# One-hot terms made on Pool, row pairs and more whole-block loads in a softmax-minus-one-hot kernel

## The chip, the cores and the metric

One core of a Trainium2 chip runs the whole program. The metric is device time in microseconds (us), the median of several executions of one compiled kernel; lower is better. The engines named here are VectorE (DVE), ScalarE (ACT), GpSimd (Pool), SyncE (SP, which only issues loads here) and the sixteen DMA engines that move data between HBM, where the inputs and outputs lie, and SBUF, the core's own memory of 128 partitions. PSUM is a second, smaller memory of the core. TensorE does two tiny transposes and plays no part. A "row" below is a tile row: 128 partitions of 8192 fp32 values, 4.19 MB. There are 64 of them, in 32 blocks of two.

## The reference

```python
logits: (8, 1024, 8192) float32;  labels: (8, 1024) int
logits_max = np.max(logits, axis=-1, keepdims=True)
exp_logits = np.exp(logits - logits_max)
softmax = exp_logits / np.sum(exp_logits, axis=-1, keepdims=True)
one_hot[batch_idx, seq_idx, labels] = 1.0
return (softmax - one_hot).astype(np.float32)
```

The kernel reads 268.5 MB and writes 268.4 MB. Both are needed by any kernel that goes over the data once.

## The kernel before

Three slots of SBUF hold one block each. SP issues loads and ACT issues stores; a load waits until the stores of the block that had its slot are done. Per row, DVE takes the maximum, ACT the exponential with its sum, DVE the reciprocal, ACT scales the whole row, and DVE subtracts "column number equals label", reading the column numbers from PSUM. The letter string says which blocks come as two one-row loads (r) and which as one whole load (w).

```python
G = 2
SLOTS = 3
LOADS = "rrrrrwwwwwwwwwwwwwwwwwwwwwrrrrrr"
# ... (set-up cut)
for t in range(T):
    x = row(t)
    label = lab[:, t % G, t // G : t // G + 1]
    w = run(nc.scalar, [w_max], act, "activation",
            out=x, in_=x, func=Act.Exp, bias=m[:, t : t + 1], scale=1.0, accum_out=s[:, t : t + 1])
    w_sum = run(nc.vector, [w], dve, "reciprocal", out=r[:, t : t + 1], in_=s[:, t : t + 1])
    if t + 1 < T:
        if (t + 1) % G == 0:
            load((t + 1) // G)
        w_max = row_max(t + 1)              # DVE: the next row's maximum
    if t > 0:
        store(t - 1)
    n = 1 if t + 1 < T else 2               # the last row in two halves
    # ... (cols: n equal slices of the row)
    scaled = [run(nc.scalar, [w_sum], act, "activation",
                  out=x[:, c], in_=x[:, c], func=Act.Copy, bias=0.0, scale=r[:, t : t + 1]) for c in cols]
    for c, w in zip(cols, scaled):
        w = run(nc.vector, [w], dve, "scalar_tensor_tensor",
                out=x[:, c], in0=iota[:, c], scalar=label, in1=x[:, c],   # iota lies in PSUM
                op0=Alu.is_equal, op1=Alu.subtract, reverse1=True)
    finished.append(w)
```

## Time and profile before

| | before |
|---|---|
| time, median of the first 3 runs (lowest to highest) | 1248.09 us (1247.36 to 1248.12) |
| span of the profiled execution | 1245.6 us |
| bytes moved, mean rate | 536.98 MB, 431 GB/s |
| busy: DVE, ACT, Pool | 1115.9, 919.0, 7.4 us |

The lines behind this table are in the prediction below. One part of the page is kept for a comparison later: the DMA issues, with the median time from issue to landing at the end of each line.

```profile
out_dram<-X ACTq DMA_DIRECT2D x64, 4096.0 KB, 30.9
X<-in_logits_dram SPq DMA_DIRECT2D x22, 4096.0 KB, 27.5
X<-in_logits_dram SPq DMA_DIRECT2D x21, 33.2
```

A store of one row needs 9.7 us of the sixteen engines at 434 GB/s, yet it lands after 30.9. The rest is queueing: this is what a transfer-bound kernel looks like from the side of one transfer.

### The profile page before, as it was taken

How to read it: one execution, taken by the hardware profiler on the slowest of the kernel's cores; microseconds unless marked ns; L12 is line 12 of the kernel's file. 1: busy time of each engine (PE TensorE's matmuls, PEld its weight loads, DVE VectorE, ACT ScalarE, POOL GpSimd, SP SyncE). 2: the span in 40 equal slices, each digit the busy share in tenths (PEclk: the TensorE clock that was granted, in tenths of full speed). 3: DMA queues.
4: the chain of work that ended last, by engine and by line, in shares of the span. 5: the costliest groups of instructions: out<-in, count | busy, mean ns of one | idle time of the engine just before them, and what ended most of it. 6: DMA issues, size and time to landing. Idle time of an engine off the chain costs nothing.

```text
span 1245.6 us, 592 instructions
## 1 busy us (share of the span) xinstructions
PE 0.4 (0%) x2; PEld 0.3 (0%) x2; DVE 1115.9 (90%) x196; ACT 919.0 (74%) x194; POOL 7.4 (1%) x7
## 2 busy tenths in 40 slices
PE   0000000000000000000000000000000000000000
PEld 0000000000000000000000000000000000000000
DVE  4999997888988889888898888988889999999893
ACT  3888886678767787767867678777777788887772
POOL 2000000000000000000000000000000000000000
DMA  9999999999999999999999999999999999999998
GB/s 398 427 428 432 437 436 441 436 431 425 426 438 448 432 416 440 431 436 438 426 446 437 418 434 432 435 437 442 425 427 438 430 429 437 435 431 431 436 434 388
DMA packets 15460, 536.98 MB, mean 431 GB/s; under 512 B 1728, under 2 KB 1728, under 8 KB 1760
## 3 DMA queue, kind: packets, MB, share of 16 engines
q1 hardware_dynamic: 6240, 268.50, 50.0%
q10 hardware_dynamic: 9216, 268.44, 49.9%
q14 instruction: 4, 0.03, 0.0%
HBM read 268.50 MB, written 268.44 MB: 431 GB/s over the span
## 4 chain that ended last, share of the span: by engine, by line
DMA 60%; DVE 37%; ACT 1%; DVEq 0%; issue 0%; ACTq 0%; SPq 0%
DMA X<-in_logits_dram 32%; DMA out_dram<-X 28%; DVE m L68 19%; DVE X L68 18%; ACT X L68 1%; DVEq L56 0%; DVE r L68 0%; ACTq L68 0%; SPq L223 0%; SPq L56 0%
## 5 line engine op out<-in xcount | busy, mean ns | idle before, releaser
L68 DVE TENSOR_REDUCE m<-X 128x1 f32<-128x8192 f32 x64 | 555.2, 8674 | 108.5 <-DMA X<-in_logits_dram 108.5
L68 ACT ACTIVATE X<-X,m 128x8192 f32<-128x8192 f32 x64 | 455.8, 7122 | 190.2 <-DVE m L68 190.2
L68 DVE SCALAR_TENSOR_TENSOR X<-iota,lab,X 128x8192 f32<-128x8192 int16 (+1 forms) x65 | 559.6, 8611 | 4.1 <-ACT X L68 4.1
L68 ACT ACTIVATE X<-X,r 128x8192 f32<-128x8192 f32 (+1 forms) x65 | 456.0, 7016 | 115.4 <-DVE r L68 115.4
L68 ACT ACTIVATION_READ_ACCUMULATOR X<-X,m 128x1 f32 x64 | 12.0, 187 | 0.0
L68 DVE RECIPROCAL r<-s 128x1 f32<-128x1 f32 x64 | 9.8, 153 | 1.7 <-ACT X L68 1.7
L68 POOL IOTA X<- 128x8192 int16 x1 | 6.9, 6943 | 0.0
L68 DVE TENSOR_SCALAR iota<-X 128x4096 int32<-128x4096 int32 x1 | 4.4, 4428 | 0.1
L68 ACT ACT_TABLE_LOAD x1 | 1.3, 1283 | 0.9 <-SPq L56 0.9
L68 DVE COPY lab<-iota 128x64 f32<-128x64 f32 x1 | 0.2, 225 | 0.5 <-PE iota L68 0.5
L68 PE MATMUL iota<-ident,lab_f 32*128 32x32 f32 x2 | 0.4, 299 | 22.4 <-DVE lab_f L68 22.4
L68 DVE CAST lab_f<-lab_raw 32x256 f32<-32x256 int32 x1 | 0.4, 363 | 0.0
L68 PEld LDWEIGHTS iota<-ident,lab_f 32*128 32x128 f32 x2 | 0.3, 193 | 22.4 <-DVE lab_f L68 22.4
L68 POOL TENSOR_SCALAR_AFFINE_SELECT ident<-ident 32x32 f32<-32x32 f32 x1 | 0.2, 203 | 0.1
L68 POOL MEMSET ident<- 32x32 f32 x1 | 0.1, 115 | 0.5 <-SPq L56 0.5
L212 POOL MEMSET const-bfloat16-1.0<- 128x1 bf16 x1 | 0.1, 106 | 0.0
L212 POOL MEMSET const-uint8-127<- 128x1 uint8 x1 | 0.1, 106 | 0.0
L212 POOL MEMSET const-float32-0.0<- 128x1 f32 x1 | 0.1, 103 | 0.2 <-issue 0.2
L212 POOL MEMSET const-float32-1.0<- 128x1 f32 x1 | 0.1, 103 | 0.0
## 6 DMA issues: line engine op xcount, KB each, us to landing
out_dram<-X ACTq DMA_DIRECT2D x64, 4096.0 KB, 30.9
X<-in_logits_dram SPq DMA_DIRECT2D x22, 4096.0 KB, 27.5
X<-in_logits_dram SPq DMA_DIRECT2D x21, 33.2
lab_raw<-in_labels_dram SPq DMA_DIRECT2D x1, 64.0 KB, 12.3
```

Of the source, the lines that this page charges most:

```text
L68: instruction = getattr(engine, method)(**operands)
L212: nc = _bacc.Bacc("TRN2", target_bir_lowering=False, num_devices=1)
```

## The change

Its intent is to take work from ACT and to shorten a row's way from load to store. Pool makes, ahead of time, the one-hot terms (0 or 1, one byte) of 6144 of the 8192 columns. One DVE pass then scales these columns and subtracts the terms at once, so ACT scales only the other 2048 columns, which DVE finishes as before. Rows are handled in pairs, both maxima first. More blocks are loaded whole, labels load on ACT's queue, and the set-up tiles borrow space of the third slot.

```diff
+HOT = 6144
+CHUNK = 1024
-LOADS = "rrrrrwwwwwwwwwwwwwwwwwwwwwrrrrrr"
+LOADS = "rrwwwwwwwwwwwwwwwwwwwwwwwwwwwrrr"
+    chunk_iota = const.tile([P, CHUNK], i16)
+    hot = const.tile([P, 2, HOT], mybir.dt.uint8)
 ... (set-up cut)
+        def row_hot(t):
+            for k in range(0, HOT, CHUNK):
+                first = [w_chunk, w_turned] if t == 0 else [w_used[t - 2]] if t > 1 else []
+                w = run(nc.gpsimd, first if k == 0 else [], pool, "tensor_scalar",
+                    out=hot[:, t % 2, k : k + CHUNK], in0=chunk_iota[:],
+                    scalar1=float(k), scalar2=label(t), op0=Alu.add, op1=Alu.is_equal)
+            w_hot[t] = w
 ...
+        def row_finish(t, w_exp):
+            w_sum = run(nc.vector, [w_exp], dve, "reciprocal", ...)
+            w_rest = run(nc.scalar, [w_sum], act, "activation",
+                out=x[:, rest], in_=x[:, rest], func=Act.Copy, bias=0.0, scale=r[:, t : t + 1])
+            w_used[t] = run(nc.vector, [w_hot[t], w_sum], dve, "scalar_tensor_tensor",
+                out=x[:, hot_cols], in0=x[:, hot_cols], scalar=r[:, t : t + 1], in1=hot[:, t % 2, :],
+                op0=Alu.mult, op1=Alu.subtract)
+            finished[t] = run(nc.vector, [w_rest], dve, "scalar_tensor_tensor",
+                out=x[:, rest], in0=iota[:], scalar=label(t), in1=x[:, rest],
+                op0=Alu.is_equal, op1=Alu.subtract, reverse1=True)
 ...
+        for b in range(B):
+            load(b)
+            row_hot(b * G)
+            row_hot(b * G + 1)
+            t = b * G
+            row_max(t)
+            row_max(t + 1)
+            if t > 0:
+                store(t - 1)
+            w = row_exp(t)
+            row_finish(t, w)
+            w = row_exp(t + 1)
+            store(t)
+            row_finish(t + 1, w)
```

More of the change, by code (lines that the diff above doesn't have):

```diff
@@ L10 @@
 SLOTS = 3
-LOADS = "rrrrrwwwwwwwwwwwwwwwwwwwwwrrrrrr"
-STORES = "rrrrrrrrrrrrrrrrrrrrrrrrrrrrrrrr"
+HOT = 6144
+CHUNK = 1024
+LOADS = "rrwwwwwwwwwwwwwwwwwwwwwwwwwwwrrr"
 @with_exitstack
@@ L36 @@
     B = T // G
+    REST = V - HOT
     lab_bp = labels.rearrange("a b -> (a b)").rearrange("(b q) -> b q", q=G * P)
@@ L45 @@
     X = const.tile([P, SLOTS, G, V], fp32)
-    lab_raw = const.tile([B, G * P], labels.dtype)
-    lab_f = const.tile([B, G, P], fp32)
-    ident = const.tile([B, B], fp32)
     lab = const.tile([P, G, B], fp32)
     m, s, r = (const.tile([P, T], fp32, name=n) for n in ("m", "s", "r"))
-    iota = psum.tile([P, V], i16)
+    chunk_iota = const.tile([P, CHUNK], i16)
+    hot = const.tile([P, 2, HOT], mybir.dt.uint8)
+    iota = psum.tile([P, REST], i16)
     lab_ps = iota[:].bitcast(fp32)[:, :T].rearrange("p (j b) -> p j b", j=G)
-    with tc.tile_critical():
+    early = X[:, SLOTS - 1, 0, :]
+    lab_raw = early.bitcast(labels.dtype)[:B, : G * P]
+    at = G * P * mybir.dt.size(labels.dtype) // 4
+    lab_f = early[:B, at : at + G * P].rearrange("b (p j) -> b j p", j=G)
+    ident = early[:B, at + G * P : at + G * P + B]
+    made = X[:, SLOTS - 1, G - 1, :].bitcast(i16)[:, :REST]
+    with tc.tile_critical(no_gpsimd_drain=True):
         sem = tc.alloc_semaphore
-        got = [[sem(f"got{i}{q}") for q in range(2)] for i in range(SLOTS)]
-        put = [[sem(f"put{i}{q}") for q in range(2)] for i in range(SLOTS)]
+        got = [[sem(f"got{i}{j}") for j in range(G)] for i in range(SLOTS)]
+        put = [[sem(f"put{i}{j}") for j in range(G)] for i in range(SLOTS)]
         lab_got, dve, act, pe, pool = (sem(n) for n in ("lab_got", "dve", "act", "pe", "pool"))
@@ L74, in run @@
             return counter, count[counter.name]
-        every, rows = slice(0, P), slice(0, G)
-        PIECES = {
-            "r": [(every, slice(j, j + 1)) for j in range(G)],
-            "h": [(slice(i, P, 2), rows) for i in range(2)],
-            "w": [(every, rows)],
-        }
-        def meets(a, b):
-            sets = [[set(range(*d.indices(n))) for d, n in zip(p, (P, G))] for p in (a, b)]
-            return all(x & y for x, y in zip(*sets))
-        loaded, stored, finished = {}, {}, []
@@ L91 @@
-        last_made = []
-        def load(b, behind_first=lambda: None):
-            loaded[b] = []
-            before = stored.get(b - SLOTS, last_made if b == SLOTS - 1 else [])
-            for q, piece in enumerate(PIECES[LOADS[b]]):
-                ps, js = piece
-                free = [w for other, w in before if meets(piece, other)]
-                w = run(
-                    nc.sync, free, got[b % SLOTS][q], "dma_start",
-                    out=X[ps, b % SLOTS, js, :], in_=x_b[b, ps, js, :],
-                )
-                loaded[b].append((piece, w))
-                if q == 0:
-                    behind_first()
@@ L107, in store @@
-        def store(t):
-            b, j = divmod(t, G)
-            stored.setdefault(b, [])
-            for q, piece in enumerate(PIECES[STORES[b]]):
-                ps, js = piece
-                if js.stop != j + 1:
-                    continue
-                w = run(
-                    nc.scalar, [finished[t]], put[b % SLOTS][q], "dma_start",
-                    out=o_b[b, ps, js, :], in_=X[ps, b % SLOTS, js, :],
-                )
-                stored[b].append((piece, w))
-        def row(t):
-            return X[:, t // G % SLOTS, t % G, :]
@@ L124, in row_max @@
-        def row_max(t):
-            b, j = divmod(t, G)
-            arrived = [w for piece, w in loaded[b] if meets(piece, (every, slice(j, j + 1)))]
-            return run(
-                nc.vector, arrived, dve, "tensor_reduce",
-                out=m[:, t : t + 1], in_=row(t), axis=mybir.AxisListType.X, op=Alu.max, negate=True,
-            )
-        w_raw = []
-        load(0, lambda: w_raw.append(run(nc.sync, [], lab_got, "dma_start", out=lab_raw[:], in_=lab_bp)))
-        w_max = row_max(0)
@@ L136 @@
-        w = run(nc.gpsimd, [], pool, "memset", ap=ident[:], constant=0.0)
+        w_raw = run(nc.scalar, [], lab_got, "dma_start", out=lab_raw, in_=lab_bp)
+        w = run(nc.gpsimd, [], pool, "memset", ap=ident, constant=0.0)
         w_ident = run(
             nc.gpsimd, [w], pool, "affine_select",
-            out=ident[:], in_=ident[:], compare_op=Alu.not_equal, fill=1.0,
+            out=ident, in_=ident, compare_op=Alu.not_equal, fill=1.0,
             base=0, pattern=[[-1, B]], channel_multiplier=1,
@@ L141 @@
         )
-        made = X[:, SLOTS - 1, G - 1, :].bitcast(i16)[:, :V]
         w_made = run(
-            nc.gpsimd, [], pool, "iota", out=made, pattern=[[1, V]], base=0, channel_multiplier=0
+            nc.gpsimd, [], pool, "iota",
+            out=made, pattern=[[1, REST]], base=HOT, channel_multiplier=0,
+        )
+        w_chunk = run(
+            nc.gpsimd, [], pool, "iota",
+            out=chunk_iota[:], pattern=[[1, CHUNK]], base=0, channel_multiplier=0,
         )
         step = mybir.dt.size(labels.dtype) // 4
-        lab32 = lab_raw[:].bitcast(i32).rearrange("b (p j s) -> b j p s", j=G, s=step)
@@ L149 @@
-        w_lab = run(nc.vector, w_raw, dve, "tensor_copy", out=lab_f[:], in_=lab32[:, :, :, 0])
+        lab32 = lab_raw.bitcast(i32).rearrange("b (p j s) -> b j p s", j=G, s=step)
+        w_lab = run(nc.vector, [w_raw], dve, "tensor_copy", out=lab_f, in_=lab32[:, :, :, 0])
         for j in range(G):
@@ L152 @@
                 nc.tensor, [w_ident, w_lab], pe, "transpose",
-                out=lab_ps[:, j, :], in_=lab_f[:, j, :], identity=ident[:],
+                out=lab_ps[:, j, :], in_=lab_f[:, j, :], identity=ident,
             )
@@ L159, with load @@
         )
-        last_made.append(((every, slice(G - 1, G)), w_iota))
-        for t in range(T):
+        loaded, stored, finished = {}, {}, {}
+        def load(b):
+            i = b % SLOTS
+            parts = [slice(0, G)] if LOADS[b] == "w" else [slice(j, j + 1) for j in range(G)]
+            for q, js in enumerate(parts):
+                rows = [b * G + j for j in range(*js.indices(G))]
+                free = [stored[t - SLOTS * G] for t in rows] if b >= SLOTS else []
+                free += [w_iota] if b == SLOTS - 1 else []
+                w = run(
+                    nc.sync, free, got[i][q], "dma_start", out=X[:, i, js, :], in_=x_b[b, :, js, :]
+                )
+                loaded.update((t, w) for t in rows)
@@ new lines, in store, with row, label @@
+        def store(t):
+            b, j = divmod(t, G)
+            i = b % SLOTS
+            stored[t] = run(
+                nc.scalar, [finished[t]], put[i][j], "dma_start", out=o_b[b, :, j, :], in_=X[:, i, j, :]
+            )
+        def row(t):
+            return X[:, t // G % SLOTS, t % G, :]
+        def label(t):
+            return lab[:, t % G, t // G : t // G + 1]
+        w_max, w_sum, w_hot, w_used = {}, {}, {}, {}
+        def row_hot(t):
+            for k in range(0, HOT, CHUNK):
+                first = [w_chunk, w_turned] if t == 0 else [w_used[t - 2]] if t > 1 else []
+                w = run(
+                    nc.gpsimd, first if k == 0 else [], pool, "tensor_scalar",
+                    out=hot[:, t % 2, k : k + CHUNK], in0=chunk_iota[:],
+                    scalar1=float(k), scalar2=label(t), op0=Alu.add, op1=Alu.is_equal,
+                )
+            w_hot[t] = w
@@ L164, with row_max, row_exp @@
+        def row_max(t):
+            w_max[t] = run(
+                nc.vector, [loaded[t]], dve, "tensor_reduce",
+                out=m[:, t : t + 1], in_=row(t), axis=mybir.AxisListType.X, op=Alu.max, negate=True,
+            )
+        def row_exp(t):
             x = row(t)
-            label = lab[:, t % G, t // G : t // G + 1]
-            w = run(
-                nc.scalar, [w_max], act, "activation",
+            return run(
+                nc.scalar, [w_max[t]], act, "activation",
@@ L168 @@
                 out=x, in_=x, func=Act.Exp, bias=m[:, t : t + 1], scale=1.0, accum_out=s[:, t : t + 1],
             )
-            w_sum = run(nc.vector, [w], dve, "reciprocal", out=r[:, t : t + 1], in_=s[:, t : t + 1])
-            if t + 1 < T:
-                if (t + 1) % G == 0:
-                    load((t + 1) // G)
-                w_max = row_max(t + 1)
+        def row_finish(t, w_exp):
+            x = row(t)
+            hot_cols, rest = slice(0, HOT), slice(HOT, V)
+            w_sum = run(nc.vector, [w_exp], dve, "reciprocal", out=r[:, t : t + 1], in_=s[:, t : t + 1])
+            w_rest = run(
+                nc.scalar, [w_sum], act, "activation",
+                out=x[:, rest], in_=x[:, rest], func=Act.Copy, bias=0.0, scale=r[:, t : t + 1],
+            )
+            w_used[t] = run(
+                nc.vector, [w_hot[t], w_sum], dve, "scalar_tensor_tensor",
+                out=x[:, hot_cols], in0=x[:, hot_cols], scalar=r[:, t : t + 1], in1=hot[:, t % 2, :],
+                op0=Alu.mult, op1=Alu.subtract,
+            )
+            finished[t] = run(
+                nc.vector, [w_rest], dve, "scalar_tensor_tensor",
+                out=x[:, rest], in0=iota[:], scalar=label(t), in1=x[:, rest],
+                op0=Alu.is_equal, op1=Alu.subtract, reverse1=True,
+            )
@@ L175 @@
+        for b in range(B):
[5 more added lines that the diff above has]
+            row_max(t + 1)
             if t > 0:
                 store(t - 1)
-            n = 1 if t + 1 < T else 2
-            cols = [slice(i * V // n, (i + 1) * V // n) for i in range(n)]
-            scaled = [
-                run(
-                    nc.scalar, [w_sum], act, "activation",
-                    out=x[:, c], in_=x[:, c], func=Act.Copy, bias=0.0, scale=r[:, t : t + 1],
-                )
-                for c in cols
-            ]
@@ L187 @@
-            for c, w in zip(cols, scaled):
-                w = run(
-                    nc.vector, [w], dve, "scalar_tensor_tensor",
-                    out=x[:, c], in0=iota[:, c], scalar=label, in1=x[:, c],
-                    op0=Alu.is_equal, op1=Alu.subtract, reverse1=True,
-                )
-            finished.append(w)
+            w = row_exp(t)
[3 more added lines that the diff above has]
+            row_finish(t + 1, w)
         store(T - 1)
-        for b in range(B - SLOTS, B):
-            for _, w in stored[b]:
-                nc.scalar.wait_ge(*w)
+        for t in range(T - SLOTS * G, T):
+            nc.sync.wait_ge(*stored[t])
```

## The prediction

> **What bounds the kernel now.** I read, in this order: the page's busy shares, its 40 slices, the two DMA queues, the chain that ended last, the groups by line, the waits of the queue that issues the loads, and the windows of the two ends. The busy shares mislead, because VectorE (DVE) leads them with 90%:
>
> ```profile
> PE 0.4 (0%) x2; PEld 0.3 (0%) x2; DVE 1115.9 (90%) x196; ACT 919.0 (74%) x194; POOL 7.4 (1%) x7
> DMA  9999999999999999999999999999999999999998
> DMA packets 15460, 536.98 MB, mean 431 GB/s; under 512 B 1728, under 2 KB 1728, under 8 KB 1760
> q1 hardware_dynamic: 6240, 268.50, 50.0%
> q10 hardware_dynamic: 9216, 268.44, 49.9%
> DMA 60%; DVE 37%; ACT 1%; DVEq 0%; issue 0%; ACTq 0%; SPq 0%
> ```
>
> The reader is to see that loads (q1) and stores (q10) together fill 99.9% of the sixteen DMA engines' time, with 9 in all slices but the last, where DVE has 8s. DVE does wait, and always for a load:
>
> ```profile
> L68 DVE TENSOR_REDUCE m<-X 128x1 f32<-128x8192 f32 x64 | 555.2, 8674 | 108.5 <-DMA X<-in_logits_dram 108.5
> L68 ACT ACTIVATE X<-X,m 128x8192 f32<-128x8192 f32 x64 | 455.8, 7122 | 190.2 <-DVE m L68 190.2
> L68 DVE SCALAR_TENSOR_TENSOR X<-iota,lab,X 128x8192 f32<-128x8192 int16 (+1 forms) x65 | 559.6, 8611 | 4.1 <-ACT X L68 4.1
> ```
>
> A load waits for its slot: the load queue spent 684.6 + 447.3 us waiting for stores to finish. So transfers, DVE and slots form one loop; the part without slack is the transfers. The windows say how little idleness is left (length, busy of five engines, clock, DMA share, GB/s):
>
> ```profile
> 0.00:2.00 2.00, 0.00 (x0) 0.00 (x0) 0.00 (x0) 1.09 (x1) 1.18 (x7) 1.00 0.23 66
> 50.00:62.00 12.00, 0.00 (x0) 0.00 (x0) 12.00 (x2) 10.89 (x2) 0.00 (x0) 1.00 0.94 407
> 500.00:750.00 250.00, 0.00 (x0) 0.00 (x0) 223.30 (x38) 185.23 (x38) 0.00 (x0) 1.00 1.00 434
> 1228.00:1230.00 2.00, 0.00 (x0) 0.00 (x0) 2.00 (x1) 0.00 (x0) 0.00 (x0) 1.00 0.91 393
> 1240.00:1244.00 4.00, 0.00 (x0) 0.00 (x0) 0.00 (x0) 0.00 (x0) 0.00 (x0) 1.00 0.59 254
> 1244.00:1246.00 2.00, 0.00 (x0) 0.00 (x0) 0.00 (x0) 0.00 (x0) 0.00 (x0) 1.00 0.00 0
> ```
>
> At 434 GB/s, the rate of the middle, 536.98 MB take 1237.3 us. The span is 1245.6, so 8 us are not transfer: about 1.6 before the first packets, 0.7 between 50 and 62 us, a few tenths at 1228, and about 3.5 after the last packets near 1242.4. A change that removes no bytes can win at most the middle two, some 1 to 2 us.
>
> **What the Trainium skill says.** (1) "DMA: Bandwidth & Descriptors", section "Where 436 GB/s comes from", puts the ceiling of the sixteen ports at 435.2 GB/s. The trace agrees: 433 to 435 in every long middle window. (2) The same page, "Queues, rings and completion order": each DMA engine alternates between queues packet by packet. Both queues show 144 packets per large DMA (9216 / 64 stores; (6240 - 48) / 43 loads), so a block loaded whole has packets twice as large and should get more than half of the engine beside a one-row store. The trace leans that way: a whole block of 8.39 MB lands in 33.2 us (253 GB/s), a row of 4.19 MB in 27.5 us (152 GB/s), a store in 30.9 us. (3) "SBUF — State Buffer", "Who interferes with whom": a DVE instruction with two SBUF inputs and a Pool instruction that reads SBUF exclude each other[...]; tensor_reduce never contends[...]. The kernel before cannot show it: its second input lies in PSUM and Pool is idle. (4) "GPSIMD Engine Reference", "Elementwise — side-by-side cycle accounting": about 1.03 cycles per element for a short one-input body, about 2.6 for two inputs, at 1.2 GHz. The trace has only the iota: 8192 int16 in 6943 ns, 0.85 ns each.
>
> **The change part by part.** Bytes: none removed. 268.44 MB in and out stay, so 1237 us stay.
>
> *ACT.* It scales 2048 columns, not 8192. From 7.12 us for 8192 and 3.69 for 4096 the slope is 0.84 ns and the fixed part 0.26 us, so 2.0 us: 5.1 us saved per row, 328 us in all. ACT goes from 919 to about 590 us. None of it is on the transfers' path; it only shortens the way from max to store.
>
> *DVE.* One pass of 8192 (8.74 us; 4.44 for 4096, so 1.05 ns per column plus 0.14) becomes one of 6144 (6.6 us) and one of 2048 (2.3 us). A row is 8.67 max + 0.15 reciprocal + 6.6 + 2.3 = 17.7 us, against 17.6 now (17.3 start to start, as neighbours overlap). For two rows 35.4, plus about 0.8 us where the second reciprocal waits for the second exp, which ACT starts only after the first row's rest: about 36. The transfers of two rows need 16.78 MB / 434 GB/s = 38.7 us. DVE keeps 2.5 us of slack per pair and still waits for loads.
>
> *Pool.* 384 new instructions of 1024 columns, 12 per pair. At 0.85 ns per column an instruction is 0.9 us and a pair 11 us; at 2.6 cycles it is 2.2 us and a pair 27 us. The two 6144-column passes may shut Pool out for 13.2 us of the pair, leaving 38.7 - 13.2 = 25.5 us. I take 1.0 to 1.8 us (estimate between the page's two figures, as there are two operations and two conversions but one input): 12 to 22 us per pair, and it fits. The other way round DVE waits at most for the Pool instruction that has just begun: after the first row's pass its buffer is free and Pool starts again, so about one instruction's remainder per pair, 0.5 to 1.5 us, inside the slack of 2.5.
>
> *Row pairs.* Both maxima go ahead of the first row's finish. From the start of the first max the first row's store is issued after about 27 us (two maxima 17.4, reciprocal, 6.6, 2.3; ACT issues it after the second exp), the second's after 36. Three blocks turn over in 3 x 38.7 = 116 us, so 80 us are left for a store (9.7 us alone, 50 at worst now) and a load (33): tight but enough; waiting stores keep the queue full.
>
> *Start.* Labels load on ACT's queue and are turned before the first max. First data come at 13.38 us now; block 2 waits for the iota copy, done by about 10 us, while rows 0 to 3 occupy the engines until about 41. Store 0 is issued near 40 us (46.8 now). Gain 0 to 0.7 us.
>
> *End.* Now the last load lands at 1200.4, store 62 is issued 17.4 us later and store 63 at 30.4. After: max 8.7, reciprocal, 6.6, 2.3, with exp of row 63 beside it, so store 62 at 18 to 19; then 0.2 + 6.6 + 2.3, so store 63 at about 28. Two stores' worth (19 us) now waits in the queue when the last load lands; with as much, the gap vanishes and up to 0.5 us is won. If the blocks loaded whole leave less behind, up to 9 us of idle engines come back here.
>
> Sum: 1245.6 - 0.5 (start) - 0.3 (end) + about 1 (partial chance of a hole at the end) is 1246 of span; the time is some 1.8 us above the span (1247.4 against 1245.6). I put **1247**.
>
> **The rivals.** *A, Pool becomes the bound.* Speaks for it: two operations, int16 in, uint8 out, shut out by DVE. At 2.2 us it just fits; at 3 us a pair needs 36 + 13 = 49 us less some overlap and the kernel would be near 1500. Against: the chunks of 1024 show that the lock was thought of. Chance of over 2% about 5%. *B, DVE becomes the bound.* 36 us plus Pool's remainders over 38.7 makes each further microsecond per pair cost 31 us: 1260 to 1290. It needs more than 2.5 us of waits per pair; 4% for more than 2%. *C, the loop of slots.* The first store of a pair comes later than with single rows, and a whole load waits for two stores; if both queues run dry together, 2 to 10 us come on top, mostly at the end. About 25%, within 2%. *D, a gain of over 2%.* It needs 461 GB/s or so over the span; no long window shows more than 435.
>
> **Range and chances.** Everything stays within a few us unless A or B holds. The floor is 1237.3 + 1.6 + 3.5 + 1.8 = 1244, less a little for the rate; the high end takes C or a light B: 1242 to 1262. Faster 0.02, same 0.90, slower 0.08.
>
> **What would show it right or wrong.** Right: DMA still 9 in nearly all slices, 433 to 435 GB/s in the middle; ACT near 590 us, DVE near 1130 us and still waiting for loads; passes of 6.6 and 2.3 us; 384 Pool instructions of 1.0 to 1.8 us; waits of DVE on Pool under 1.5 us per pair. Wrong: DMA shares below 9 in the middle with DVE waiting for Pool (A), 6144-column passes much longer than 6.6 us or DVE above 97% (B), idle engines between 1210 and 1235 us (C), or a middle rate away from 434, which would break the ground of the whole sum.

## The result, and the profile after

The changed kernel takes **1887.79 us** (median of 6 runs, 1886.94 to 1887.98), against 1247.76 us (6 runs, 1247.14 to 1248.52) for the kernel before. The ratio is 1.5127, with a 95% interval of 1.5108 to 1.5147. Ratios here and below are the mean time of one kernel's fast runs over that of the other's of the same rounds, so not quite the ratio of the medians. The result is correct; the kernel is 51% slower.

From the page of the changed kernel: the busy shares, the slices of Pool and of the transfers, the two queues, the chain that ended last, and the groups (busy us, mean ns of one, idle time ahead and who ended it).

```profile
PE 0.4 (0%) x2; PEld 0.3 (0%) x2; DVE 1125.3 (60%) x259; ACT 587.6 (31%) x193; POOL 1825.1 (97%) x392
POOL 9999999999999999999999999999999999999995
DMA  9976786567866668666687666786566868666324
q1 hardware_dynamic: 5328, 268.44, 34.9%
q10 hardware_dynamic: 9264, 268.51, 33.3%
POOL 97%; issue 2%; DVE 1%; DMA 0%; PE 0%; ACTq 0%; DVEq 0%; SPq 0%
...
L77 POOL TENSOR_SCALAR hot<-chunk_iota,lab 128x1024 uint8<-128x1024 int16 x384 | 1821.9, 4744 | 37.5 <-DVE lab L77 1.8
L77 DVE SCALAR_TENSOR_TENSOR X<-X,r,hot 128x6144 f32<-128x6144 f32 x64 | 424.1, 6627 | 734.5 <-POOL hot L77 734.5
L77 DVE TENSOR_REDUCE m<-X 128x1 f32<-128x8192 f32 x64 | 552.7, 8676 | 7.0 <-DMA X<-in_logits_dram 7.0
...
out_dram<-X ACTq DMA_DIRECT2D x64, 4096.0 KB, 11.1
```

The reader is to see a bound that has moved. Before, the transfers stood at 9 in all slices but the last and DVE waited 108.5 us for loads. Now the transfers are at 5 to 8 in all but the first and last slices, a store lands in 11.1 us because nothing queues in front of it, DVE waits 7 us for loads, and Pool is busy without a break. DVE's own work has hardly grown (1125 against 1116 us); its 734.5 us of waiting are all for Pool.

What a row costs Pool is read from the chain of waits in the middle of the changed kernel (start us, duration us, what):

```profile
607.75 3.70 POOL hot L77
611.45 0.09 issue
611.55 10.12 POOL hot L77
...
621.75 3.70 POOL hot L77
...
636.93 3.70 POOL hot L77
640.63 0.09 issue
640.73 10.12 POOL hot L77
```

Beside it, the DVE passes of the same stretch in the timeline:

```profile
611.56 6.62 DVE L77 SCALAR_TENSOR_TENSOR X<-X,r,hot 128x6144 f32<-128x6144 f32 x1 [3.05 <-POOL hot L77]
640.74 6.62 DVE L77 SCALAR_TENSOR_TENSOR X<-X,r,hot 128x6144 f32<-128x6144 f32 x1 [20.23 <-POOL hot L77]
```

A plain Pool instruction takes 3.70 us and 0.09 us to the next. One in six takes 10.12 us: it starts together with a DVE pass of 6.62 us and is longer by 6.42 us, nearly the whole pass. A row therefore costs 6 x 3.796 + 6.42 = 29.2 us, a pair 58.4, and the timeline shows 58.4 from pair to pair (reciprocals at 608.36 and 666.72). Pool starts at 5.9 us; 64 rows of 22.8 us and 62 shut-outs of 6.42 us end at 1863 us, where its last instruction does end, and 22 us of finishing and storing follow. That is the whole span. What is not yet shown is why one instruction costs 3.70 us, whether the 6.42 us are a shut-out (Pool kept from SBUF while DVE reads there), and whether anything else in the change costs time.

### The profile page after: what moved, and what is told of

Same layout as the page of the kernel before. It is cut to its first block, busy times and chain, and to the rows that moved or that the text cites. A ratio compares the mean times of both kernels' runs of the same rounds, so it can differ in the third digit from the quotient of the medians.

```text
span 1885.2 us, 1103 instructions
## 1 busy us (share of the span) xinstructions
PE 0.4 (0%) x2; PEld 0.3 (0%) x2; DVE 1125.3 (60%) x259; ACT 587.6 (31%) x193; POOL 1825.1 (97%) x392
## 4 chain that ended last, share of the span: by engine, by line
POOL 97%; issue 2%; DVE 1%; DMA 0%; PE 0%; ACTq 0%; DVEq 0%; SPq 0%
POOL hot L77 97%; DVE X L77 0%; DMA X<-in_labels_dram 0%; PE iota L77 0%; DVE lab L77 0%; ACTq L233 0%; DVEq L76 0%; SPq L65 0%
## 5 line engine op out<-in xcount | busy, mean ns | idle before, releaser
L77 POOL TENSOR_SCALAR hot<-chunk_iota,lab 128x1024 uint8<-128x1024 int16 x384 | 1821.9, 4744 | 37.5 <-DVE lab L77 1.8
L77 DVE SCALAR_TENSOR_TENSOR X<-X,r,hot 128x6144 f32<-128x6144 f32 x64 | 424.1, 6627 | 734.5 <-POOL hot L77 734.5
L77 ACT ACTIVATE X<-X,r 128x2048 f32<-128x2048 f32 x64 | 128.1, 2001 | 147.9 <-DVE r L77 147.9
L77 DVE SCALAR_TENSOR_TENSOR X<-iota,lab,X 128x2048 f32<-128x2048 int16 x64 | 150.1, 2345 | 0.0
## 6 DMA issues: line engine op xcount, KB each, us to landing
out_dram<-X ACTq DMA_DIRECT2D x64, 4096.0 KB, 11.1
```

The source lines that it names most:

```text
L77: instruction = getattr(engine, method)(**operands)
```

## The experiments

The theory: Pool's own instruction time plus the time that DVE's passes shut it out is the whole loss, and with Pool relieved the transfers bound the kernel again. The rivals: row pairs and whole loads break the overlap of loads and stores (slots); the passes over 6144 columns are slow for reading SBUF twice; the long Pool instruction is slow for a reason of its own. Runs with a single timed execution are used for effects far above 1% and for durations in their traces.

### What one Pool instruction costs (m_pool)

```diff
 (the kernel before, after its set-up)
+for src, kind, n, ops, val in TRIES:       # 20 kinds, four of each
+    w = run(nc.gpsimd, [w], pool, "tensor_scalar", out=d[kind][:, :n], in0=src[:, :n], **how)
```

> The kernel before, with 80 Pool tensor_scalar instructions added whose results nobody reads (20 kinds, four of each): input int16 or fp32, output uint8, int16, bf16 or fp32, 256 to 1024 columns, one or two operations, label or immediate. The time should stay 1247 to 1250 us, since Pool is idle there and nothing waits for it. What is asked is what makes the 1024-column instruction of the changed kernel take 3.70 us. Theory dtypes (integer input and one-byte output are converted in slow code): the fp32 to fp32 kinds take 1.0 to 1.5 us and the int16 to uint8 kinds with one operation stay near 3.7. Theory operations (each operation is paid per element): one operation takes about half of 3.7 whatever the types. Theory fixed cost: 256 columns take nearly as long as 1024.

Measured: 1247.58 us, correct. The idle Pool took 80 instructions without any effect on the time. The groups of Pool (each of 8 mixes four with one operation and four with two; mean ns after the comma):

```profile
L72 POOL TENSOR_SCALAR dst<-src,lab 128x1024 uint8<-128x1024 int16 x8 | 26.2, 3275 | 0.8
L72 POOL TENSOR_SCALAR dst<-src,lab 128x1024 f32<-128x1024 f32 x8 | 26.2, 3275 | 0.8
L72 POOL TENSOR_SCALAR dst<-src,lab 128x512 uint8<-128x512 int16 x4 | 8.0, 1997 | 0.4
L72 POOL TENSOR_SCALAR dst<-src,lab 128x512 f32<-128x512 f32 x4 | 6.3, 1563 | 0.4
L72 POOL TENSOR_SCALAR dst<-src,lab 128x256 uint8<-128x256 int16 x4 | 4.6, 1144 | 0.4
```

The theory of types falls: int16 to uint8 and fp32 to fp32 have the same mean to the nanosecond. The theory of a fixed cost falls too: 256 columns take 1.14 us and not 3.7. In the timeline single instructions of 1024 columns show 3.71 or 3.72 us with two operations and 2.84 or 2.85 with one. With two operations 512 columns take 2.00 us and 256 take 1.14; with one, 512 take 1.56. So two operations cost (3.72 - 2.00) / 512 = 3.36 ns per column, one costs (2.84 - 1.56) / 512 = 2.50, and some 0.28 us are fixed. An operation is then 0.86 ns per column; taken back to no operation, 1.64 ns per column are left, twice what the iota of the kernel before needs in all (0.85). The theory of operations holds in part only: going from two to one saves 23%, not half. The compare is not to blame: four instructions with one addition took 2.77 us each.

### Is the long instruction a shut-out? (e_psum, e_write2)

```diff
-                out=..., in0=x[:, hot_cols], scalar=r[:, t : t + 1], in1=hot[:, t % 2, :],
+                out=..., in0=x[:, hot_cols], scalar=r[:, t : t + 1], in1=iota[:, hot_cols],   # PSUM, all 8192 columns
```

> The changed kernel with the second input of the 6144-column pass taken from PSUM in place of Pool's terms in SBUF; DVE still waits for Pool's terms, and the result is wrong on purpose. Theory shut-out (the one instruction per row that takes 10.12 us is held for the whole pass, because both read SBUF): all Pool instructions take 3.70 us, a row costs 6 x 3.796 = 22.8 us and the time falls to 1460 to 1490 us. Rival (the sixth instruction is slow for another reason, such as waiting for its buffer): still near 1885 us.

Measured: 1491.84 us, 2 us above the stated range, wrong result as intended. Pool's 384 instructions:

```profile
L77 POOL TENSOR_SCALAR hot<-chunk_iota,lab 128x1024 uint8<-128x1024 int16 x384 | 1422.3, 3704 | 36.8 <-DVE lab L77 1.0
```

The mean fell from 4744 to 3704 ns and the longest is 3708. In the loop only DVE's second input was changed, from one-byte terms in SBUF to column numbers in PSUM (for which the set-up makes 8192 of them and not 2048), the pass still took 6.62 us, and DVE still waited for Pool's terms, so the 6.42 us per row are a shut-out by a pass with two inputs in SBUF. It accounts for 1887.8 - 1491.8 = 396 us; the other 242 us over the kernel without Pool's work (1250.1, below) are Pool's own 22.8 us per row.

The other side of the rule is a Pool that only writes.

```diff
-                    nc.gpsimd, first if k == 0 else [], pool, "tensor_scalar", ...
+                    nc.gpsimd, first if n == 0 else [w], pool, "memset", ap=hot[:, t % 2, k : k + CHUNK], constant=0,
 (twelve memsets per row in place of six tensor_scalar)
```

> The refused kernel, mended: each memset waits for the one before. Pool clears the tile of terms (12 memsets of 1024 columns per row) in place of computing them; result wrong on purpose. Same waits on DVE, but Pool only writes SBUF. If the shut-out holds only against Pool instructions that read SBUF, all memsets take their plain time (0.3 to 1.0 us) also during the 6144-column passes; if any Pool access is shut out, some take up to 6.6 us longer. Time 1245 to 1256 us in either case, as Pool has time to spare.

Measured: 1253.16 us (a run of the kernel before beside it: 1248.6). All 768 memsets took 951 or 952 ns and all passes 6.617 to 6.620 us, although some memsets ran inside passes: a series of 24 ran from 607.38 to 631.41 us, with a pass from 610.03 to 616.65:

```profile
607.38 24.03 POOL L77 MEMSET hot<- 128x1024 uint8 x24 [14.14 <-DVE X L77]
610.03 6.62 DVE L77 SCALAR_TENSOR_TENSOR X<-X,r,hot 128x6144 f32<-128x6144 f32 x1
```

These Pool instructions, which only write SBUF, are not shut out. They also write the tile that the pass reads from, so sharing that tile is not what holds Pool. Two single runs cannot tell whether the 0.4% in time are real.

### Does the rest of the change cost anything? (e_nopool, e_loads)

```diff
+        w_zero = run(nc.gpsimd, [], pool, "memset", ap=hot[:], constant=0)
         def row_hot(t):
-            for k in range(0, HOT, CHUNK): ...      # Pool's six instructions
+            w_hot[t] = w_zero
 (the loop is emptied)
```

> The changed kernel without Pool's 384 instructions: the tile of one-hot terms is cleared once and DVE passes read it (result wrong on purpose in 6144 columns, the label's one is missing). Everything else, row pairs, whole loads, 6144-column passes, ACT's rest of 2048, stays. Pool theory: with Pool's work gone nothing else stands in the way, DVE needs about 36 us per pair against 38.7 of transfers, and the time is 1243 to 1256 us. Rival (row pairs and whole loads cost time of their own, or the 6144-column passes are slower for reading SBUF twice): above 1270 us.

Measured, wrong result as intended: 1250.1 us (4 runs), ratio 1.0018 (1.0005 to 1.0032). The window from 500 to 750 us (length; busy us of PE, PEld, DVE, ACT, Pool; clock; DMA share; GB/s) shows the transfers back at their limit:

```profile
500.00:750.00 250.00, 0.00 (x0) 0.00 (x0) 226.25 (x51) 114.37 (x37) 0.00 (x0) 1.00 1.00 432
```

The passes took 6619 ns. Row pairs, the additional whole loads and the two-input pass together cost 0.2%. This is the cleanest of the runs: of the 640 us lost, all but 2 to 3 us went with Pool's instructions.

```diff
 (the kernel before)
-LOADS = "rrrrrwwwwwwwwwwwwwwwwwwwwwrrrrrr"
+LOADS = "rrwwwwwwwwwwwwwwwwwwwwwwwwwwwrrr"
```

> The kernel before with the changed kernel's order of loads alone: blocks 2 to 28 whole, 0, 1 and 29 to 31 as rows. If whole loads break the overlap, some per cent slower; if transfers are full either way, 1244 to 1252 us, the same within half a per cent.

Measured: 1252.12 us (5 runs), ratio 1.0032 (1.0018 to 1.0046). The order of loads alone costs the kernel before 0.3%, as far as its interval goes; the time is 0.1 us above the expected range.

### How many columns may Pool take? (e_hot2048 to e_hot5120)

The edit is one number in each: `HOT = 6144` becomes 2048, 3072, 4096 or 5120.

> The changed kernel with 2048 hot columns in place of 6144, all else kept: row pairs, whole loads, ACT scaling the rest. Pool theory (Pool's own instructions plus the time DVE shuts it out are the whole loss): a row costs Pool 2 x 3.8 + 2.2 = 9.8 us, below the 19.3 us that the transfers of a row take, so the time falls to 1243 to 1252 us. Slot theory (pairs and whole loads break the overlap of loads and stores): it stays above 1300 us.

Measured: 1376.5 us (4 runs), ratio 1.1035. This is a miss for the Pool theory, whose range ended at 1252 us: Pool was busy only 35% of the span, yet the transfers did not bound it either. The slot theory named such a time (above 1300 us), but not for the reason that the trace shows: DVE waited for loads only 2.5 us in the whole run. The chain of waits of this run in its middle names the reason:

```profile
604.02 15.91 DVE m L77 x2
...
621.12 0.17 DVE r L77
...
621.31 12.43 ACT X L77 x2
...
634.06 5.42 ACT X L77
639.48 0.02 issue
639.50 6.62 DVE X L77
```

In the pair order, ACT scales the first row's rest before it starts the second exp, and scales the second row's rest after that. With a rest of 6144 columns (5.42 us) nothing hides this: 42.1 us from pair to pair (604.02 to 646.12), against 38.7 for the transfers. So the size of the hot part has two sides: a small one lengthens the chain of DVE and ACT, a large one lengthens Pool's work. A later run, made when the time with 4096 columns was known, tests that chain with a number put together in advance.

> The changed kernel with 3072 hot columns: a test of the chain of DVE and ACT that bounded 2048 (42.1 us per pair). Put together from measured pieces: maxima 15.9 beyond the overlap, 1.4, ACT's rest 4.6 and the second exp 7.1, 0.3, ACT's rest again 4.6, the pass of 5120 columns 5.5: 39.4 us per pair, against 38.7 of transfers; with the 29 us of ends that the run with 2048 shows beside 32 pairs this is about 1290 us (1270 to 1300). Pool with 3 instructions per row is far from a bound.

Measured: 1287.88 us, correct, with 39.3 us from pair to pair in the chain (604.69 to 644.02). The expected time was about 1290.

> The changed kernel with 4096 hot columns. Pool theory: a row costs Pool 4 x 3.796 + 4.3 = 19.5 us, 39.0 per pair. Chain theory (2048 hot columns were slow because ACT's scaling of the first row's rest, 3.7 us here, stands between the two exps): 17.3 + 1.4 + 3.7 + 7.3 + 0.2 + 4.4 + 4.4 = 38.7 us per pair. Both are beside the 38.7 of the transfers, so 1250 to 1290 us, far below both neighbours (1376 at 2048 and 1888 at 6144).

Measured: 1249.85 us, correct, 0.15 us below the stated range. In the window from 500 to 750 us the transfers run at 431 GB/s and Pool is busy 214.74 of 250 us:

```profile
500.00:750.00 250.00, 0.00 (x0) 0.00 (x0) 227.94 (x51) 135.06 (x37) 214.74 (x54) 1.00 1.00 431
```

> The changed kernel with 5120 hot columns: a third point for the sum of Pool's time. Pool theory: a row costs 5 x 3.796 + (5120-column pass of 5.5 less 0.2) = 24.3 us, and 64 rows plus 17 us of ends are 1570 us, if Pool is shut out for a whole pass in each row; if only one of the two passes of a pair meets it, 1400 to 1420.

Measured: 1522.39 us, correct: between the two stated cases. The chain shows why: the shut-outs alternate, 9.05 us for one instruction and 7.17 for the other of a pair.

```profile
610.02 9.05 POOL hot L77
619.07 0.09 issue
...
634.35 3.70 POOL hot L77
638.05 0.09 issue
638.15 7.17 POOL hot L77
```

The other pass, of the next pair's first row, began at 636.20 us, 1.85 us into the plain instruction of 634.35, which still took 3.70 us; the pass still took 5.55. Only the next Pool instruction was held, until the pass ended. The sum with these two values, 10 x 3.796 + 5.35 + 3.47 = 46.8 us per pair, agrees with Pool's series (6.1 to 1498.9 us in 32 pairs: 46.7).

| hot columns | Pool per pair, us | DVE and ACT chain per pair, us | transfers per pair, us | time, us |
|---|---|---|---|---|
| 2048 | 15.2 | 42.1 | 38.7 | 1376.5 |
| 3072 | 22.8 | 39.3 | 38.7 | 1287.9 |
| 4096 | 34.5 | 37.3 | 38.7 | 1249.9 |
| 5120 | 46.8 | not read | 38.7 | 1522.4 |
| 6144 | 58.4 | 35.6 (e_write2) | 38.7 | 1887.8 |

Pool's column is instructions times 3.796 us plus the shut-outs that the traces show (none at 2048 and 3072; 8 x 0.52 at 4096, from the mean of 4223 ns). The chain at 4096 is from 619.84 to 657.18 us; the one at 6144 is put together from two pieces of the timeline (17.4 from the first maximum to the first pass, 18.2 from there to the end of the second row). The largest of three numbers in a line sets the time, and only at 4096 is it the transfers'.

### Fewer operations, and the best of both (e_oneop, e_oneop4096, e_4096loads)

```diff
+lab_k = labels less 0, 1024, 2048, ... (made once)
-    scalar1=float(k), scalar2=label(t), op0=Alu.add, op1=Alu.is_equal,
+    scalar1=<column of lab_k>, scalar2=None, op0=Alu.is_equal,
 (m, s, r become rings of eight columns to make room)
```

> The changed kernel with one operation per Pool instruction: labels less 0, 1024, ... are made once, and a chunk is is_equal against those; result right. Statistics are kept in rings of eight columns to make room. If the cost is paid per operation, an instruction takes 1.9 to 2.3 us, a row costs Pool 6 x 2.1 + 6.4 = 19 us, and the time falls to 1250 to 1330 us. If the cost lies in the types or in the compare, an instruction stays above 3.3 us and the time above 1700 us.

Measured: 1401.71 us, correct, and outside both stated ranges: an instruction takes 2.84 us (as m_pool says), not 2.1. Still bounded by Pool, 98% busy. The timeline shows something new here:

```profile
602.21 13.04 POOL L78 TENSOR_SCALAR hot<-chunk_iota,lab_k 128x1024 uint8<-128x1024 int16 x3
605.15 7.40 DVE L78 SCALAR_TENSOR_TENSOR X<-X,r,hot 128x6144 f32<-128x6144 f32 x1 [6.12 <-POOL hot L78]
```

Now DVE's pass takes 7.40 us, 0.78 longer than 6.62. Two plain Pool instructions of 2.84 us ran from 602.21 to 607.84 us, so the second had begun near 605.0, just ahead of the pass. It held DVE for 0.78 us and not for its whole length, and the third was held until the pass ended.

The kept traces, read pass by pass, show when this happens. If a pass begins 1.06 us or more after the Pool instruction that is running, it is not lengthened (1.85 us in the run of 5120, for instance). If it begins sooner, the extra time always ends 0.90 or 0.91 us after that instruction's start: 0.12 us after it the pass was longer by 0.78 (here), 0.38 us after it by 0.52 (once in the changed kernel), 0.79 us after it by 0.12 (31 passes of the run of 3072), 0.82 us after it by 0.08 (the run of one operation with 4096 columns). So a Pool instruction of 1024 columns holds such a pass off only in its first 0.9 us, with one operation as with two; what it does in this time is not shown. Which of the two goes first when they begin together cannot be read from their starts: a Pool instruction that began 0.04 us after the pass held it for 0.94 us (the pass of 632.10 us here), one that began 0.01 us before it was itself held (the changed kernel).

> 4096 hot columns and one operation per Pool instruction. Pool: 4 x 2.93 + 4.3 = 16 us per row, 32 per pair, below the transfers; the chain of DVE and ACT is 38.7 as in the run with two operations. 1246 to 1275 us; below the run with two operations by up to 20 us if Pool bounded that one, equal to it if the chain did.

Measured: 1250.25 us (4 runs), ratio 1.0019 (1.0006 to 1.0033), the same as with two operations (1249.85): Pool was no bound at 4096 columns, and freeing it further (64% busy) gave nothing.

> 4096 hot columns with the order of loads of the kernel before (blocks 5 to 25 whole). With the changed order this was 1249.85 us in one run; the order of loads alone cost the kernel before 0.3%. If that part adds up, 1244 to 1248 us, the same as the kernel before within 0.3%; a gain of more than 0.5% would show that the shorter way of a row is worth something after all.

Measured: 1248.72 us (5 runs), ratio 1.0008 (0.9994 to 1.0022): the same as the kernel before, though 0.7 us above the stated range. ACT's busy time is 696.9 us, 24% less than before, and the time is the same. No version beat the kernel before.

## Why the prediction was right or wrong

**What bounds the kernel now: right.** Whenever Pool and the chain stay below 38.7 us per pair, the time comes back to 1248 to 1253 us with 431 to 434 GB/s in the middle (e_nopool, e_write2, e_hot4096, e_oneop4096, e_4096loads).

**The sum: wrong in one term.** The step that failed is "I take 1.0 to 1.8 us (estimate between the page's two figures, as there are two operations and two conversions but one input): 12 to 22 us per pair, and it fits." The instruction took 3.70 us and 0.09 to the next, so 12 of them take 45.6 us per pair. This alone exceeds the 38.7 us of the transfers. The prediction took the duration from figures for other bodies and bracketed it with the only Pool row in the trace, an iota, which has no input and no compare. Both sides of the bracket were too low: 2.2 us, its slowest case, is 60% of the measured duration.

**The shut-out: right in size, and it matters more than said.** It was put at 13.2 us per pair; the trace shows 2 x 6.42 = 12.8. The whole size came only because Pool was the bound, so that nearly every pass began together with a Pool instruction; with 4096 columns, where it was not, the two passes of 9.0 us per pair shut Pool out for 4.2. With the right duration the prediction's own formula for rival A gives 45.6 + 12.8 = 58.4 us per pair, the measured value. So the mechanism that decided the case was on the list, with 5%, and the chance was wrong because it hung on the one duration that the trace before could not show. "Less some overlap" was wrong for 6144 columns: in the middle there was none, since each pass waits for the last term and starts when Pool starts the next.

**"The chunks of 1024 show that the lock was thought of": no evidence.** Such a guess about an author speaks for nothing; it was used against rival A.

**ACT, DVE, passes: right.** 587.6 us for ACT against 590, 1125.3 for DVE against 1130, passes of 6.62 and 2.35 us against 6.6 and 2.3, 2.00 us for ACT's rest. The 36 us of a pair's chain are 35.6 in e_write2.

**Rival B, DVE as the bound: no.** DVE waited on Pool for a term to be finished, not for its own capacity. The 0.5 to 1.5 us per pair by which Pool was to hold DVE up did not appear in the changed kernel (passes of 6.62 us); with one operation they were 0.78 + 0.94 us.

**Rival C, the loop of slots: small.** e_nopool puts everything but Pool at 0.2%; whole loads alone cost 0.3% in the kernel before. The ways at the two ends were read rightly: in e_nopool the first store is issued at 42.8 us (46.8 before, near 40 predicted) and the last two 17.7 and 27.0 us after the last load (18 to 19 and 28 predicted). The gain of 0.8 us set against it did not show in the time.

**Rival D, a large gain: no**, as said; no run was faster than the kernel before.

**Slips that changed nothing.** A gain of 2% needs 431 x 1.02 = 440 GB/s over the span, not 461; it is still more than any long window shows. These windows run from 432 (1000 to 1150 us) to 435, not from 433. After the last packets 3.2 us are left and not 3.5, and the idle pieces named add up to about 6 of the 8 us. The last row's half passes took 4.48 us each; 4.44 is half of their 8.88 together, in which they overlap. DVE waited for loads, but not always: 5.8 us of its waits were for ACT. That a block loaded whole gets more than half of the engines is not shown either: with more of them and nothing else changed (e_loads) a store lands in 28.6 us, not later than the 30.9 before.

## What to carry to other kernels

Before moving work to an idle engine, ask for the duration of exactly that instruction on that engine, and where no trace has it, give the estimate a wide range (here an iota of 1024 columns took 0.97 us on Pool and this instruction 3.70, a factor of nearly four) and give the rival its share of the chance; or time the instruction first, beside a kernel in which that engine is idle, as m_pool did at no cost. Then compare every engine's time per unit of work, shut-outs included, with the bound: relieving ACT was worth nothing here, since the transfers set the pace, while the new load on Pool had only 25 us per pair to fit into. A split between engines has two sides, and the table above shows how narrow the good part can be: 1288 us, 1250 us, 1522 us for steps of 1024 columns.

## What the Trainium skill lacked or had wrong

- "GPSIMD Engine Reference", sections "Elementwise — side-by-side cycle accounting" and "Engine selection": the first gives about 1.03 cycles per element for bodies with k up to 2 (read here as operations) and about 2.6 for two inputs, the second calls one-input work roughly line-rate. Here tensor_scalar with one tensor input takes 2.50 ns per column with one operation and 3.36 ns with two, 3.0 and 4.0 cycles at the page's 1.2 GHz, plus about 0.28 us, and input and output types make no difference. The page has no row for tensor_scalar, and its figures do not carry over to it.
- "SBUF — State Buffer", section "Who interferes with whom": it says that a DVE instruction with two SBUF inputs contends with a Pool instruction that reads SBUF and not with one that only writes it. The runs agree (a pass of 6.62 us holds a reading Pool instruction for 6.42; all 768 memsets took 951 to 952 ns). How long such a pair hold each other it does not say: that the first has the shared ports for its whole instruction stands there for DVE's 2-port modes. Here DVE held Pool to the end of its pass, but Pool held DVE only until 0.90 us after its own start, of 2.84 or 3.70 us.
